# Longer pauses and finer steps for the lanes of small products in a two-layer hybrid backbone

## The chip, the cores and the metric

The kernel runs on one core of a Trainium2 chip. The metric is the device time of one execution in microseconds. Times shown are medians of a few runs; the profile is of one further execution of the same program.

## The reference

Two layers work on 1024 latent tokens and 256 context tokens of width 1024. The even layer runs latent attention (8 heads) and a chunked gated linear attention (GLA, 4 heads, both directions) side by side. The odd layer is a chunked gated DeltaNet (8 heads, both directions) with a short convolution of three taps on q, k and v. Each layer has modulated norms before both halves and a squared-ReLU MLP of width 4096. Cut to what the change touches:

```python
# GLA, per chunk of 64 and head (b = cumulative sum of the log gates)
q_dec, k_inv = q * exp(b), k * exp(-b)
a = where(incl, q_dec @ k_inv^T, 0);  o = a @ v + q_dec @ s
s = s * exp(b_end)[:, None] + (k * exp(b_end - b))^T @ v

# gated DeltaNet, per chunk of 64 and head
a_mat = where(strict, (k * beta) @ k^T * decay, 0) + eye(64)
sol = triangular_solve(a_mat, [v * beta, k * beta * exp(g)])

def rms_norm(x, w):
    return x * rsqrt(mean(x * x) + EPS) * w
```

## The kernel before

Large products run as three fp32r products per 128-wide contraction step (high by high, low by high, high by low; `mm3`, L180 to L183). `group` (L185) runs the eight steps of one 512-token block into one PSUM buffer. Its argument `every` says after how many microseconds of product columns it calls `pump`, at 1e9 once at the end of the group; `rate` scales the budget that `pump` hands on.

The rest of the work is written as generators, the lanes: GLA, norms, the feeders of the DeltaNet, the inversion of its triangular matrices. `lanes` (L58) lists them. `pump(us)` (L60) goes through the list, and each lane runs until what it yields adds up to the budget times its weight. A lane that yields `None` ends its turn for this call: that is a pause. What a lane records in its turn stands on each engine's queue at this place among the large products. The tile framework then orders the instructions of each engine; the order of the built program is shown below where it matters.

The places that the change touches:

- `stat_lane` (L233): squares (ScalarE), their sums, then a pause (L245), then the products `st` with a column of ones, then `rsqrt_small` on VectorE. `norm_lane` (L269) pauses once (L274) and then spreads the result with products `rb`.
- `gla_gates` (L333) computes gates on ScalarE, GpSimd and VectorE (a scan, L355), scales `gq` and `gk`, and transposes `gab` into `gkn` (L385). `gla_main` (L401) makes `pa` (L417), the state products `pk` (L435), the chain of states `gst` on VectorE (L439) and the outputs `po` (L457, L460). `gla_tail` (L473) normalises and transposes (L486). All of them share four PSUM buffers.
- In layer 1, `dense1` (L1136) runs the input projections. `conv_out` (L1164) accumulates the three taps on VectorE (L1174). `qk_lane` (L1189) transposes a projected block (L1198), normalises it, transposes it back (L1218) and stores it. `v_lane` (L1223) transposes (L1230) and stores.
- `decay_lane` (L1311) makes the decays of five sets of matrices with the products `pG` (L1327). `inv_lane` (L1358) makes the products `pk` (L1372), multiplies them on VectorE (L1375), and inverts the 32 by 32 diagonal blocks there: a transpose into `X` (L1390), thirty steps of two instructions that depend on each other (L1396, L1398), two transposes into `U` (L1407). `inv_tail` (L1420) joins the blocks with the products `pq` (L1429) and `pu` (L1441). These lanes share four PSUM buffers, tag `t`; the projections have four of their own.
- Five of the eight `gates` projections follow the last v block, then the lanes are drained, then three more `gates` projections cover the loads of the scan, whose first product is `pa` of L1628.

```python
            t += 3 * n / 2400
            if t >= every or k == nk - 1:
                pump(t * rate)
                t = 0.0
```

Of the kernel before, what the change touches and what calls it, by code (L numbers as in the profile page):

```python
# [33 lines left out]
def hybrid_backbone(ctx: ExitStack, tc: tile.TileContext, a, out, taps=None):  # L34
# [44 lines left out]
    def complete(gen):  # L79
        run(gen)  # L80
        lanes[:] = [it for it in lanes if it[0] is not gen]

    def run(gen):
# [149 lines left out]
    def stat_lane(hs, c0, n, tp, small, pp, ptag, dim, inc=False, engs=(V, G)):  # L233

        acc = []
        for i, h in enumerate(hs):
            sq = tp.tile([128, 512], F32, name="sq", tag="t")
            S.activation(out=sq[:, :n], in_=h[:, c0:c0 + n], func=AF.Square)
            if len(acc) < (1 if inc else 2) or (inc and i == len(hs) - 1):
                acc.append(sq)  # L240
            else:
                x = acc[0 if inc else i % 2]
                engs[i % 2].tensor_tensor(out=x[:, :n], in0=x[:, :n], in1=sq[:, :n], op=ALU.add)
            yield 0.4
        for _ in range(2 if inc else 1):  # L245
            yield None
        nt = n // 128
        st = pp.tile([128, 512], F32, name="st", tag=ptag)
        last = None
        for t in range(nt):  # L250
            for i, x in enumerate(acc):
                last = after(PE.matmul(st[:, t:t + 1], x[:, t * 128:(t + 1) * 128], ones, start=(i == 0), stop=(i == len(acc) - 1)), last)
        r = rsqrt_small(small, st[:, :nt], nt, dim)
        yield 1.2
        return r
# [13 lines left out]
    def norm_lane(hs, c0, n, A, B, dst, tp, small, pp, ptag, r=None, inc=False, rb=None, ks=range(KD)):  # L269

        c = 0 if c0 < LAT else 1
        if r is None and rb is None:
            r = yield from stat_lane(hs, c0, n, tp, small, pp, ptag, D, inc)
            yield None  # L274
        if rb is None:
# [125 lines left out]
    def gla_main(g):  # L401
# [3 lines left out]
        for h in range(4):  # L405
            while ("qk", h) not in gla:
                yield None
            qd, ki, v = gla["load", h]
            A_ = g.sb.tile([128, NT, 128], F32, name="gA")
            for t0 in (0, 4, 8):  # L410
# [18 lines left out]
            for s0 in (0, 8, 16):  # L429
                pk = [g.pp.tile([128, 4, 128], F32, name="pk", tag="p") for _ in range(2)]  # L430
                n = min(8, 19 - s0)
# [14 lines left out]
            ssq = g.sm.tile([128, NT], F32, name="gssq")  # L446
            yield None
            for t0 in (8, 0, 4):
# [24 lines left out]
    def gla_tail(g, h, o, ssq):  # L473
# [3 lines left out]
        yield 2.8  # L477
        yield None
        while ("gs", h) not in gla:
# [653 lines left out]
    with ExitStack() as e1:  # L1133
        pp = pool(e1, "pp1d", 4, space=PSUM)

        def dense1(chunks, blocks, rate=0.75, every=1e9, between=None):  # L1136
            ws = [w1s.pop() if w1s else load_w(a["owT"][m], wm[0], wbufs=2) for m, _ in chunks]
# [8 lines left out]
        with ExitStack() as e2:  # L1146
# [42 lines left out]
            def qk_lane(y, nt, gain, m, key):  # L1189

                yield None
                nat = cv.tile([128, NT, 128], F32, name="nat", tag="nat")
                ssq = small.tile([128, NT, 2], F32, name="ssq")
                for t0 in range(0, nt, 4):
# [6 lines left out]
                    S.activation(out=sq[:, :n], in_=pt[:, :n, :], func=AF.Square)  # L1201
                    V.tensor_reduce(out=ssq[:, t0:t0 + n], in_=sq[:, :n].rearrange("p t (a d) -> p t a d", a=2), axis=AX.X, op=ALU.add)
                r = rsqrt_small(small, ssq[:, :nt].rearrange("p t h -> p (t h)"), nt * 2, 1, gain)
                n3 = nat[:, :nt].rearrange("p t (a d) -> p (t a) d", a=2)
                V.tensor_tensor(out=n3, in0=n3, in1=r.unsqueeze(2).to_broadcast([128, nt * 2, 64]), op=ALU.mult)
                if key:
                    for p in range(2):
                        for a_ in range(2):
                            nc.sync.dma_start(out=d_X[m][64 * a_:64 * a_ + 64, p::2, 1, :],
                                              in_=nat[64 * p:64 * p + 64, :, 64 * a_:64 * a_ + 64])  # L1210
                for _ in range(3):
                    yield None
                xT = cv.tile([128, T], F32, name="xT", bufs=1)
                for t0 in range(0, nt, 4):
                    n = min(4, nt - t0)
                    pt = ptp.tile([128, 4, 128], F32, name="pt", tag="t")
                    for i in range(n):
                        PE.transpose(pt[:, i, :], nat[:, t0 + i, :], ident)  # L1218
                    S.copy(out=xT[:, t0 * 128:(t0 + n) * 128], in_=pt[:, :n, :].rearrange("p t f -> p (t f)"))
                nc.sync.dma_start(out=d_X[m][:, 0:2 * nt, 0 if key else 2, :], in_=xT[:, :nt * 128].rearrange("p (c j) -> p c j", j=64))  # L1220
                state[("k" if key else "q", m)] = True

            def v_lane(y, hh):  # L1223
                yield None
                vn = cv.tile([128, NT, 128], F32, name="vn", tag="nat")
                for t0 in range(0, NT, 4):
                    n = min(4, NT - t0)
                    pt = ptp.tile([128, 4, 128], F32, name="pt", tag="t")
                    for i in range(n):
                        PE.transpose(pt[:, i, :], y[:, tok(t0 + i)], ident)  # L1230
                    S.copy(out=vn[:, t0:t0 + n], in_=pt[:, :n, :])
                for p in range(2):
                    r0 = 64 * (hh % 2)
# [77 lines left out]
            def decay_lane():  # L1311

                for s, m in enumerate(sets):
# [3 lines left out]
                    for z in range(2):  # L1317
# [5 lines left out]
                        G.tensor_tensor(out=b4(R, m), in0=bc(g_, m), in1=i2b, op=ALU.mult)  # L1323
                        yield None
                        for i in range(2):
# [94 lines left out]
            def inv_tail(m, Nv, U, Y):  # L1420
                yield None
                yield None
                Q = [Nv[:, 16 * z:16 * z + 16, 0:32] for z in range(2)]
                for z in range(2):
# [6 lines left out]
                    for p in range(2):  # L1431
                        S.copy(out=Q[z][64 * p + 32:64 * p + 64], in_=pq[64 * p + 32:64 * p + 64])
                yield None
                for z in range(2):
# [408 lines left out]
```

## Time and profile before

| what | value |
|---|---|
| median of 3 runs | 3446.05 us (3445.41 to 3446.22) |
| the profiled execution's own time | 3441.82 us |
| its span in the profile | 3440.1 us |
| mean granted clock of TensorE | 0.97 |
| TensorE busy | 3264.4 us, 95% |
| VectorE busy | 2116.4 us, 62% |
| ScalarE busy | 1173.3 us, 34% |
| GpSimd busy | 1080.7 us, 31% |

The profiled execution's time exceeds its span by 1.7 us and lies 4.2 us under the median of the runs. The shares are means over stages that have different limits. Products are pipelined, and their ends are modelled: a product of 512 columns is shown with 0.39 us, while the next one starts after less. All times of the trace count from the start of the span.

### The profile page before, as it was taken

To read this page: it belongs to the slowest core of one execution; us is meant where nothing else is said; L and a number is where in the kernel's file an instruction comes from. 1 tells how busy PE (TensorE), PEld (TensorE's weight loads), DVE (VectorE), ACT (ScalarE), POOL (GpSimd) and SP (SyncE) were. 2 spreads that over 40 slices of the span, in tenths; PEclk is the share of its full clock that TensorE was granted. 3 is DMA by queue.
4 is the path that set the end of the run, shared out by engine and by line. 5 is a ranking of instruction groups with operands and counts; after the bars stand their busy time and mean duration, and the time that the engine had idled before them with its cause. 6 is when DMAs were issued, how large, how long until landed. Compare 5 with 4: busy or idle time off the path is not lost.

```text
span 3440.1 us, 48403 instructions
## 1 busy us (share of the span) xinstructions
PE 3264.4 (95%) x18676; PEld 2709.8 (79%) x18676; DVE 2116.4 (62%) x3873; ACT 1173.3 (34%) x2158; POOL 1080.7 (31%) x805
## 2 busy tenths in 40 slices
PE   8988988999899999999999898999999999999998
PEld 4876767777688888888888786777988788888887
DVE  4757446666568777776445779783765444444445
ACT  3234245665232212121212465452664311212112
POOL 2312136677442111111111343443117422222223
PEclk8998999999899999999999999999999999999999
DMA  5633132111622222222111234346454211111111
GB/s 197 197 101 90 59 120 72 29 47 29 203 80 77 86 70 85 69 91 59 49 37 38 74 93 103 92 121 155 104 111 148 68 49 43 49 50 48 43 51 62
DMA packets 284966, 287.86 MB, mean 84 GB/s; under 512 B 156424, under 2 KB 222032, under 8 KB 284736
## 3 DMA queue, kind: packets, MB, share of 16 engines
q1 hardware_dynamic: 272928, 263.53, 26.6%
q0 software_dynamic: 5760, 10.75, 1.3%
q10 hardware_dynamic: 6048, 10.49, 1.0%
q8 instruction: 147, 2.41, 0.3%
q14 instruction: 83, 0.68, 0.1%
HBM read 231.34 MB, written 53.36 MB: 83 GB/s over the span
## 4 chain that ended last, share of the span: by engine, by line
PE 69%; DVE 11%; DMA 3%; issue 2%; ACT 2%; POOL 2%; SPq 1%; DVEq 0%; ACTq 0%; POOLq 0%
PE ps L181 18%; PE ps L182 18%; PE ps L183 18%; DVE X L1398 1%; DVE tm L1396 1%; PE S L181 1%; PE S L182 1%; PE S L183 1%; DMA adaw<-in_adaw_dram 1%; PE pa L1645 1%; DVE y L1174 1%; PE acc L875 1%; PE acc L877 1%; PE acc L876 1%; PE M L857 1%
## 5 line engine op out<-in xcount | busy, mean ns | idle before, releaser
L170 POOL TENSOR_TENSOR wlo<-wst,whi 128x1024 fp32r<-128x1024 f32 (+1 forms) x207 | 489.8, 2374 | 1635.0 <-ACT whi L167 1587.9
L167 ACT CAST whi<-wst 128x1024 fp32r<-128x1024 f32 (+2 forms) x213 | 212.6, 1012 | 845.5 <-PE ps L182 771.8
L181 PE MATMUL ps<-th,whi 128*128 128x512 f32 (+1 forms) x1304 | 479.6, 368 | 7.0 <-DVE h L1068 5.4
L183 PE MATMUL ps<-th,wlo 128*128 128x512 f32 (+1 forms) x1304 | 476.3, 365 | 2.4 <-POOL wlo L170 2.4
L182 PE MATMUL ps<-tl,whi 128*128 128x512 f32 (+1 forms) x1304 | 477.5, 366 | 0.0
L1033 DVE TENSOR_TENSOR rl<-rl 128x512 f32<-128x512 f32 (+1 forms) x160 | 214.4, 1340 | 345.1 <-ACT rl L1032 344.5
L181 PE MATMUL ps<-mxh,whi 128*128 128x512 f32 (+1 forms) x1008 | 357.8, 356 | 0.0
L182 PE MATMUL ps<-mxl,whi 128*128 128x512 f32 (+1 forms) x1008 | 352.8, 350 | 0.3 <-POOL mxl L170 0.3
L183 PE MATMUL ps<-mxh,wlo 128*128 128x512 f32 (+1 forms) x1008 | 351.8, 350 | 0.0
L126 DVE SCALAR_TENSOR_TENSOR acc<-adaw,sc,acc 128x256 f32<-128x256 f32 (+1 forms) x476 | 286.2, 643 | 55.5 <-DMA adaw<-in_adaw_dram 55.4
L1068 DVE SCALAR_TENSOR_TENSOR h<-ps,mod,h 128x512 f32<-128x512 f32 (+1 forms) x384 | 243.5, 656 | 95.1 <-PE ps L183 93.7
L181 PEld LDWEIGHTS ps<-th,whi 128*128 128x128 f32 x1304 | 246.7, 189 | 51.0 <-DVE h L1068 7.2
L183 PEld LDWEIGHTS ps<-th,wlo 128*128 128x128 f32 x1304 | 246.3, 189 | 43.6 <-POOL wlo L170 3.2
L182 PEld LDWEIGHTS ps<-tl,whi 128*128 128x128 f32 x1304 | 246.9, 189 | 38.6
L1068 DVE SCALAR_TENSOR_TENSOR g<-ps,mod,g 128x512 f32<-128x512 f32 (+1 forms) x264 | 188.5, 731 | 106.3 <-PE ps L183 106.1
L181 PEld LDWEIGHTS ps<-mxh,whi 128*128 128x128 f32 x1008 | 195.2, 194 | 26.3 <-issue 1.2
L182 PEld LDWEIGHTS ps<-mxl,whi 128*128 128x128 f32 x1008 | 195.4, 194 | 25.8 <-issue 1.4
L183 PEld LDWEIGHTS ps<-mxh,wlo 128*128 128x128 f32 x1008 | 194.9, 194 | 23.9
L932 POOL TENSOR_TENSOR pl<-P,ph 128x512 fp32r<-128x512 f32 x144 | 178.6, 1247 | 89.9 <-DVE ph L931 60.1
L183 PE MATMUL ps<-m1h,wlo 128*128 128x512 f32 x512 | 203.9, 398 | 0.0
L181 PE MATMUL ps<-m1h,whi 128*128 128x512 f32 x512 | 203.9, 398 | 0.0
L182 PE MATMUL ps<-m1l,whi 128*128 128x512 f32 x512 | 203.6, 398 | 0.0
(376 smaller groups left out, 6725.5 us busy)
## 6 DMA issues: line engine op xcount, KB each, us to landing
wst<-in_w_dram SPq DMA_DIRECT2D x128, 512.0 KB, 3.5
adaw<-in_adaw_dram SPq DMA_DIRECT2D x224, 128.0 KB, 2.1
adaw<-in_adaw_dram SPq DMA_DIRECT2D x80, 256.0 KB, 4.5
wst<-in_owT_dram SPq DMA_DIRECT2D x25, 512.0 KB, 3.6
wst<-in_ewo_dram SPq DMA_DIRECT2D x16, 512.0 KB, 3.6
wY<-d_YA SPq DMA_DIRECT2D x64, 128.0 KB, 3.2
wst<-in_owo_dram SPq DMA_DIRECT2D x16, 512.0 KB, 3.5
wst<-in_ewT_dram SPq DMA_DIRECT2D x14, 512.0 KB, 7.1
```

Of the source, the lines that this page charges most:

```text
L126: V.scalar_tensor_tensor(out=acc[c], in0=w, scalar=sc[:, k, c:c + 1], in1=acc[c], op0=ALU.mult, op1=ALU.add)
L167: S.copy(out=hi, in_=src)
L170: lo_eng.tensor_tensor(out=lo, in0=src, in1=hi.bitcast(F32), op=ALU.subtract)
L181: PE.matmul(ps, hi_w, hi_x, start=first, stop=False)
L182: PE.matmul(ps, hi_w, lo_x, start=False, stop=False)
L183: PE.matmul(ps, lo_w, hi_x, start=False, stop=last)
L857: PE.matmul(ps[:, :kn_], qh[0:96, qt * 128:(qt + 1) * 128], kh[0:96, k0:k0 + kn_], start=True, stop=True)
L875: PE.matmul(o[:, :n], vh[:, j, :], ph[:, :n], start=(j == (0 if b < 2 else NTL)), stop=False, skip_group_check=True)
L876: PE.matmul(o[0:64, :n], vl[:, j, :], ph[:, :n], start=False, stop=False, skip_group_check=True)
L932: (V if j % 4 == 3 else G).tensor_tensor(out=pl[:, :n], in0=P_[:, :n], in1=ph[:, :n].bitcast(F32), op=ALU.subtract)
L1033: V.tensor_tensor(out=r[:, :n], in0=r[:, :n], in1=r[:, :n], op=ALU.mult)
L1068: V.scalar_tensor_tensor(out=h[m][:, c0:c0 + n], in0=ps[:, :n], scalar=mod[l][:, 40 + m, c:c + 1], in1=h[m][:, c0:c0 + n], op0=ALU.mult, o ...
```

## The change

A helper `pause(n)` yields `None` n times. Most lanes that wait for another engine's result before a product get more pauses than before. The transposes of `qk_lane` and `v_lane` end the lane's turn after each group of four. `dense1` pumps after every third contraction step of a 512-column group (its `every` is 1.6 where it was 1e9). The computation is the same.

```diff
+    def pause(n):
+
+        for _ in range(n):
+            yield None
...
@@ stat_lane
-        for _ in range(2 if inc else 1):
-            yield None
+        yield from pause(3 if inc else 2)
@@ norm_lane
             r = yield from stat_lane(hs, c0, n, tp, small, pp, ptag, D, inc)
-            yield None
+            yield from pause(3)
@@ gla_main
             qd, ki, v = gla["load", h]
+            yield from pause(4)
             A_ = g.sb.tile([128, NT, 128], F32, name="gA")
...
             ssq = g.sm.tile([128, NT], F32, name="gssq")
-            yield None
+            yield from pause(2)
@@ gla_tail
         yield 2.8
-        yield None
+        yield from pause(4)
@@ dense1
-        def dense1(chunks, blocks, rate=0.75, every=1e9, between=None):
+        def dense1(chunks, blocks, rate=0.75, every=1.6, between=None):
@@ qk_lane
-                yield None
+                yield from pause(3)
...
                     V.tensor_reduce(out=ssq[:, t0:t0 + n], in_=sq[:, :n].rearrange("p t (a d) -> p t a d", a=2), axis=AX.X, op=ALU.add)
+                    yield None
...
-                for _ in range(3):
-                    yield None
+                yield from pause(5)
...
                     S.copy(out=xT[:, t0 * 128:(t0 + n) * 128], in_=pt[:, :n, :].rearrange("p t f -> p (t f)"))
+                    yield None
@@ v_lane
-                yield None
+                yield from pause(3)
...
                     S.copy(out=vn[:, t0:t0 + n], in_=pt[:, :n, :])
+                    yield None
@@ decay_lane
-                        yield None
+                        yield from pause(2)
                         for i in range(2):
                             pG = ptp.tile([128, 8, 64], F32, name="pG", tag="t")
@@ inv_tail
-                yield None
-                yield None
+                yield from pause(4)
...
-                yield None
+                yield from pause(2)
                 for z in range(2):
                     pu = ptp.tile([128, 16, 32], F32, name="pu", tag="t")
```

How the order moves, at three places. Line numbers of the changed kernel lie 4 to 7 higher than before; the number at a tile's name tells buffers apart.

TensorE, the fifth and last set's `pq` in the layer-1 projections, in the kernel before:

```order
L183 MATMUL ps<-mxh_7_7179,wlo 128x512
L1429 MATMUL pq<-U_20985,Nm 32x32 x64
L181 MATMUL ps<-m0h_0_8096,whi 128x512
L1441 MATMUL pu<-U_20984,Nm 32x32
L182 MATMUL ps<-m0l_0_8104,whi 128x512
L183 MATMUL ps<-m0h_0_8096,wlo 128x512
L1441 MATMUL pu<-U_20984,Nm 32x32 x31
L1441 MATMUL pu<-Nm,U_20984 32x32 x32
```

The same place in the changed kernel:

```order
L188 MATMUL ps<-mxh_7_8087,wlo 128x256
L1435 MATMUL pq<-U_20690,Nm 32x32 x64
L186 MATMUL ps<-m0h_0_8096,whi 128x512
L187 MATMUL ps<-m0l_0_8104,whi 128x512
L188 MATMUL ps<-m0h_0_8096,wlo 128x512
```

Before, `pq` stands among the `gates` projections, with 144 dense products between it and the scan's first `pa`. Now it stands at the end of the seventh v block (a 256-column group ends in front of it), and 384 dense products and ten transposes of the eighth v block follow it.

VectorE, the end of the fourth set's inversion (`U`) and the start of the fifth's (`X`), in the kernel before:

```order
L1407 STREAM_TRANSPOSE U_20440<-X 128x32x32
L1407 STREAM_TRANSPOSE U_20439<-X 128x32x32
L1174 SCALAR_TENSOR_TENSOR y<-ps,cw,y 128x511 x2
L1174 SCALAR_TENSOR_TENSOR y<-ps,cw,y 128x1
L1174 SCALAR_TENSOR_TENSOR y<-edge,cw,y 128x1
L1174 SCALAR_TENSOR_TENSOR y<-ps,cw,y 128x255 x2
L1375 TENSOR_TENSOR Nm<-pk,Nm 128x512 x4
L1375 TENSOR_TENSOR Am<-pk,Am 128x512 x4
L1390 STREAM_TRANSPOSE X<-Nm 128x1024
```

The same place in the changed kernel:

```order
L1414 STREAM_TRANSPOSE U_20160<-X 128x32x32
L1414 STREAM_TRANSPOSE U_20159<-X 128x32x32
L1382 TENSOR_TENSOR Am<-pk,Am 128x512 x4
L1397 STREAM_TRANSPOSE X<-Nm 128x1024
L1179 SCALAR_TENSOR_TENSOR y<-ps,cw,y 128x511
L1403 TENSOR_TENSOR tm<-X 128x30
L1179 SCALAR_TENSOR_TENSOR y<-ps,cw,y 128x511
```

The fifth set's products `Nm` now stand ahead of the fourth set's `U`, and the convolution's rows stand between the steps of the fifth inversion.

TensorE, the first GLA head (`pa`, the transposes `pt<-gab`, the next head's gates `ps<-small_t`, `pk`), in the kernel before:

```order
L181 MATMUL ps<-a0h_0_145,whi 128x512
L417 MATMUL pa<-gq,gk 128x128 x20
L385 MATMUL pt<-ident,gab 128x128 x10
L342 MATMUL ps<-small_t,gu 128x512
L435 MATMUL pk<-gvt,gkn 64x128 x16
L342 MATMUL ps<-small_t,gu 128x512
L342 MATMUL ps<-small_t,gu 128x256
```

The same place in the changed kernel:

```order
L187 MATMUL ps<-a0l_2_155,whi 128x512
L389 MATMUL pt<-ident,gab 128x128 x10
L346 MATMUL ps<-small_t,gu 128x512 x2
L346 MATMUL ps<-small_t,gu 128x256
L422 MATMUL pa<-gq,gk 128x128 x20
L440 MATMUL pk<-gvt,gkn 64x128 x32
L188 MATMUL ps<-a0h_2_147,wlo 128x512
```

The whole place lies seven dense products later, the transposes and the next head's gates come first, and `pa` and 32 of the 38 `pk` follow without a dense product between.

## Rows read from the trace of the kernel before

**Rows 1.** The profile's page: busy us (share of the span) xinstructions of each engine.

```profile
PE 3264.4 (95%) x18676; PEld 2709.8 (79%) x18676; DVE 2116.4 (62%) x3873; ACT 1173.3 (34%) x2158; POOL 1080.7 (31%) x805
```

**Rows 2.** Windows by stage: length, busy us (x) per engine, granted clock, DMA.

```profile
core 0: us, PE busy (x) PEld busy (x) DVE busy (x) ACT busy (x) POOL busy (x), PEclk, DMA share, GB/s
200.00:410.00 210.00, 178.22 (x1467) 144.55 (x1466) 126.05 (x244) 80.59 (x101) 50.17 (x37) 0.89 0.28 80
1930.00:1960.00 30.00, 22.40 (x115) 19.17 (x114) 27.80 (x43) 15.50 (x24) 12.39 (x8) 0.83 0.30 103
1995.50:2054.80 59.30, 56.84 (x410) 47.64 (x411) 45.33 (x96) 34.87 (x57) 21.49 (x10) 1.00 0.35 89
1995.50:2346.20 350.70, 322.37 (x3010) 267.66 (x3011) 293.59 (x597) 176.25 (x274) 140.73 (x96) 0.97 0.42 105
```

**Rows 3.** TensorE's waits, 1995 to 2394 us: us in total, times, longest.

```profile
PE pt L1198 <- DVE Nm L1375: 6.6, 1, 6.6
```

**Rows 4.** TensorE's waits, 205 to 420 us, the four largest.

```profile
PE pt L486 <- DVE gst L439: 8.6, 2, 4.7
PE pa L417 <- issue: 8.2, 3, 4.4
PE pa L417 <- DVE gk L374: 5.6, 1, 5.6
PE po L457 <- DVE gst L439: 3.9, 1, 3.9
```

**Rows 5.** VectorE's waits, 1995 to 2346 us, all of them.

```profile
DVE y L1174 <- ACT y L1169: 13.4, 7, 4.5
DVE U L1407 <- POOL X L1402: 8.0, 4, 3.7
DVE Nm L1375 <- PE pk L1372: 7.8, 2, 4.4
DVE y L1174 <- ACT edge L1171: 7.2, 4, 3.4
DVE ssq L1202 <- ACT sqn L1201: 7.1, 3, 5.6
DVE X L1390 <- ACT Nm L1389: 2.9, 2, 1.6
DVE Am L1375 <- PE pk L1372: 1.0, 1, 1.0
```

**Rows 6.** Timeline of VectorE, end of the fifth inversion: start, us, instruction, idle before.

```profile
2342.01 4.17 DVE L1407 STREAM_TRANSPOSE U<-X 128x1024 f32<-128x1024 f32 x2 [3.70 <-POOL X L1402]
```

**Rows 7.** Timeline of TensorE from the fifth `pq` to the scan.

```profile
2356.72 2.21 PE L1429 MATMUL pq<-U,Nm 32*32 32x32 f32 x128
...
2362.16 0.50 PE L181 MATMUL ps<-m0h,whi 128*128 128x512 f32 x1
...
2394.29 0.39 PE L1628 MATMUL pa<-wv,wY 128*128 128x128 f32 x2
```

**Rows 8.** Timeline of VectorE: a step of the inversion and a convolution row behind it.

```profile
2286.70 0.19 DVE L1398 TENSOR_TENSOR X<-X,tm 128x30 f32<-128x30 f32 x1
2286.81 0.74 DVE L1174 SCALAR_TENSOR_TENSOR y<-ps,cw,y 128x511 f32<-128x511 f32 x1
```

**Rows 9.** Timeline of VectorE, first GLA head's states and the next head's scan.

```profile
253.49 2.82 DVE L355 TENSOR_TENSOR_SCAN gab<-cm,gmn 64x1280 f32<-64x1280 f32 x1 [3.33 <-POOL gmn L349]
256.23 0.32 DVE L439 SCALAR_TENSOR_TENSOR gst<-gst,ggi,pk 128x128 f32<-128x128 f32 x1
```

**Rows 10.** Timeline of TensorE, the norm between the layers.

```profile
1936.59 0.38 PE L252 MATMUL st<-ones,sq 128*128 128x1 f32 x2 [0.99 <-DVE sq L243]
...
1952.27 1.16 PE L261 MATMUL rb<-ident,rs_y 128*128 128x128 f32 x8 [3.19 <-DVE rs_y L215]
```

**Rows 11.** Timeline of TensorE: ten transposes; one set's `pk`.

```profile
1998.29 1.25 PE L1198 MATMUL pt<-ident,y 128*128 128x128 f32 x10
...
2046.43 3.95 PE L1372 MATMUL pk<-kq 64*64 64x64 f32 x128
```

## The prediction

> **What bounds the kernel now.** I read the busy shares first. TensorE is busy for 3264.4 of 3440.1 us [rows 1], so the most that a better order could return is the missing 176 us, and only in the stages that the change reaches. The windows by stage come next. The chunked-GLA stage (200 to 410 us) has TensorE busy 178 of 210 us at a granted clock of 0.89, that is, part of it at 1.2 GHz instead of 2.4. The projection and inversion stage of layer 1, from the first `pc` product at 1995.5 us to the scan, shows something else: until 2346.2 us VectorE is busy 293.6 of 350.7 us [rows 2]. The waits say who holds whom. In the GLA stage TensorE waits 31.5 us in nine kinds of wait, nearly all for the inputs or buffers of small products; the four largest, 26.3 us, are in [rows 4]. In the inversion stage its longest wait is 6.6 us [rows 3], about 29 us over 13 kinds. VectorE's own waits there are 13.4 + 8.0 + 7.8 + 7.2 + 7.1 + 2.9 + 1.0 = 47.4 us [rows 5]. So VectorE's instructions and the issue between them fill 350.7 - 47.4 = 303.3 us, and it is the next bound of this stage, not a helper with room.
>
> The end of the stage is read from the timeline. The last two transposes into `U` run on VectorE from 2342.01 for 4.17 us [rows 6]. TensorE takes the `pq` products that read them at 2356.72, ten us after: there TensorE is late, not VectorE. From `pq` to the scan's first `pa` (2394.29) are 37.57 us: 5.44 us of `pq` and `pu`, then 141 dense products in 32.13 us, 0.228 us each [rows 7].
>
> **The change, part by part.** No engine gains or loses an instruction of weight: 16106 products stand in both orders. Only places move.
>
> *Finer steps in `dense1` (L1136).* A pump now follows every third contraction step instead of a whole group, so three pumps where one was, and each may overrun its budget by one step. The lanes therefore advance faster per dense product than before, in spite of the longer pauses. In the two orders I count dense products of 512 columns: the fifth `pq` stands before the last 144 of them in the kernel before and before the last 384, with ten transposes, in the changed one. Since `pq` cannot start before the `U` transposes, 240 x 0.228 = 54.7 us and 1.25 us (ten transposes, [rows 11]) are moved behind VectorE's last inversion step: the tail grows from 37.6 to 93.5 us.
>
> When does that last step end? VectorE's queue in front of it loses only seven convolution rows (2.9 us at the 0.74 us of a 511-column one, [rows 8], less for the narrow ones). It also becomes better mixed: the chain of the inversion (L1396, L1398) is left for another instruction 70 times before, 126 times now. A convolution row behind a chain row starts at 2286.81, before the chain row's end at 2286.70 + 0.19 [rows 8], 0.08 us saved; 56 more of them save 4.5 us. VectorE's own need is then 303.3 - 2.9 - 4.5 = 295.9 us. (The Trainium skill, VectorE: DVE Perf Modes, section "The DRAIN you can't avoid", says that the next operation does not start until the pipe is empty, whatever is chained; by it the 4.5 us would be nothing and the sum 4.5 us longer. The row speaks for an overlap between independent operations.)
>
> To this come the waits that stay. In the first 59.3 us, until the first `X`, VectorE is busy only 45.3 [rows 2], which holds some 12 of its 47.4 us of waits; the first `pk` stands after 119 dense products instead of 164, ten us sooner, and VectorE's work ahead of it shrinks as much: I keep 10. Between the second `pq` and the third set's first `pk` TensorE has 50 dense products, `pq`, `pu` and 20 transposes, 11.5 + 5.4 + 2.5 us, then 3.95 us of `pk` [rows 11] and 2 us until `X`: 25 us, for which VectorE holds some 12: 13 of wait. Of the trips to GpSimd before `U` (8.0, [rows 5]) I keep 6, since nothing is put between. Sum 29, against 47.4 now. The last pair ends at 1995.5 + 295.9 + 29 = 2320.4, its first half 2.1 earlier, at 2318.3; plus the tail, 2411.8. TensorE waits ahead of `pq`, so some dense products will run at 1.2 GHz: 3 us. The stage ends at 2414.8 instead of 2394.3: **+20.5 us**. Bounds: if VectorE never waited, 2382.8, or -11.5, excluded by the 10 us at the start, so -1.5; if it waited as now, 2433, or +39. I take the middle value, because the order shows two of the three waits and not the rest.
>
> *Pauses in the GLA lanes (L409, L447, L478).* What the pauses delay is `pa`, `po` and the tail's transposes; `pt<-gab` (L385) has no pause and comes to stand first. For head 0 it needs `gab`, one product of 1.5 us after the `gk` that `pa` waits 5.6 us for [rows 4], and stands seven dense products (1.6 us) later: the wait changes its name, not its size. Then `po`: now it waits 3.9 us for `gst`, which stands on VectorE behind a scan that waits for GpSimd [rows 9]. In the new order both scans (2 x 2.8 us) stand ahead of all `gst` steps, so `pk`'s last six products, which need a buffer that the seventh `gst` step frees, would wait some 8 us: +4. For heads 1 to 3, `pa` (8.2 us, [rows 4]) gains cover in two of three cases (-4 us), and the transposes that waited 8.6 us stand behind fewer `pk` products (-6), but the third `pa` group of heads 1 and 2 needs buffers that VectorE frees only after the next head's scans (+2 to +5 each). With a little clock back I take **-4 us**. Bounds: all of the stage's 31.5 us and the lost clock (0.11 of 210 us) gone, -54; twice the scans' 5.6 us in the way, +15.
>
> *Pauses in the statistics lanes (L245, L274).* At 1936 to 1952 us `st` waits 0.99 and `rb` 3.19 us [rows 10]. Now 24 dense products (5.5 us) stand between them instead of 13 (3.0): `rb` keeps 0.7, `st` nothing, and less runs at the 0.83 clock [rows 2]: **-3 us** (-8 to +2, since the second `st` loses cover). The norm of layer 0's second block had no wait to lose; at the very end nothing dense is left to cover with: 0.
>
> *Pauses in the inversion and its feeders (L1191, L1211, L1224, L1324, L1421, L1433, and the three that split the transposes into groups of four)* act inside the sum of the stage above; alone they would push `pq` back, the wrong way only for the lanes' speed.
>
> **Sum:** 20.5 - 4 - 3 = +13.5 us. The profiled execution took 3441.82 us, so 3455; the median of the runs shown is 4.2 us above it, so the forecast in those terms is **3460 us** (+0.4%). A change under 0.2% (7 us) is about what a measurement of this kernel cannot tell from none.
>
> **The rivals.**
> 1. *Faster: the pauses cover what they were put in for, and VectorE keeps up.* It decides at the point where VectorE waits under 12 us in the inversion stage (the +20.5 falls to +3) while the GLA waits really go (-30 with their clock) and the norm's (-6): -33, 3413 us. For it: the GLA stage has 32 of 210 us without TensorE and a clock of 0.89 [rows 2]. Against it: 295.9 us of VectorE work and 93.5 us behind it, which no pause shortens. The Trainium skill (TensorE: Matmul & The Clock Gate, section "HAM oscillation") says that each wait puts the array back to half clock, so that a removed wait returns more than itself; the clock of 0.89 agrees, and by that rule this rival gains. Chance 0.17.
> 2. *No change:* the inversion stage loses 7 to 13 and GLA and norms return as much: 3440 to 3452 us, 0.15.
> 3. *Much slower:* VectorE waits as it does now (+39) and the scans block GLA (+10): 3492 us, 0.13.
> The forecast has 0.55. That the change does not do what it says is part of 2: in the GLA stage the small products still stand right behind their feeder.
>
> **How the numbers follow.** Slower by over 0.2%: 0.55 + 0.13 = 0.68; within: 0.15; faster: 0.17. The forecast's own range is 3453 to 3485 us. The range for 8 in 10 adds rival 2, the upper part of rival 1 and the lower part of rival 3: 3434 to 3492.
>
> **What would show it.** Right: in the changed profile the fifth `pq` starts right after the last `U`, between 2305 and 2345 us on this time axis, with TensorE idle for ten us or more in front of it or in front of transposes that wait for VectorE; VectorE's busy share before it is over 0.87; and some 90 us of nearly unbroken dense work follow, with VectorE nearly idle. Wrong: the last `U` ends before 2300 us, or `pq` does not wait. For GLA: the sum of waits between 200 and 410 us stays above 20 us and `pk` or `pt<-gab` heads the list. The prediction fails if the GLA stage gets shorter by over 15 us, or if VectorE's waits in the inversion stage fall under 15 us.

## The result and the profile after

The changed kernel takes 3465.24 us (median of 4 runs, 3462.31 to 3472.89), the kernel before beside it 3445.81 us (3445.41 to 3446.22). The ratio is 1.0069, 95% interval [1.0057, 1.0082]: slower by 0.7%. The profiled execution took 3465.45 us with a span of 3463.7, so 23.6 us more than the one shown before.

Where the time goes can be read by counting. The 12048 products of `mm3` stand in the same order in both kernels, so the start of the n-th one in one trace less its start in the other is the time lost or won up to there (`pc` and `pa` are the small products that begin the layer-1 stage and the scan):

```
place                                   before     after    shift
first product                             39.9      39.0     -0.9
product 1020, behind the GLA stage       500.2     492.9     -7.4
product 2160, second block's norm        973.0     962.4    -10.6
product 6900, end of layer 0's MLP      1915.2    1907.1     -8.1
first pc, start of the layer-1 stage    1995.5    1986.4     -9.1
first pa of the scan                    2394.3    2416.4    +22.1
last instruction                        3440.1    3463.7    +23.6
```

Everything ahead of the layer-1 projections got 9.1 us faster, and the stage from `pc` to the scan 31.2 us slower (430.0 against 398.8). The shares of the whole hardly tell it:

```profile
PE 3267.5 (94%) x18676; PEld 2709.9 (78%) x18676; DVE 2123.1 (61%) x3873; ACT 1171.3 (34%) x2154; POOL 1083.3 (31%) x805
```

The windows by stage do. First the whole stage in the kernel before, then three of the changed kernel: GLA, the layer-1 stage until the last `U`, and the whole stage. The columns are those of [rows 2].

```profile
1995.50:2394.29 398.79, 370.45 (x3457) 307.41 (x3458) 305.00 (x617) 189.47 (x294) 161.16 (x119) 0.97 0.45 110
```

```profile
200.00:410.00 210.00, 182.49 (x1513) 147.28 (x1512) 127.90 (x257) 81.34 (x104) 51.83 (x38) 0.89 0.28 80
1986.40:2322.60 336.20, 289.87 (x2799) 237.20 (x2800) 296.81 (x591) 165.17 (x254) 134.63 (x96) 0.91 0.40 96
1986.40:2416.40 430.00, 383.49 (x3451) 314.82 (x3452) 310.93 (x617) 189.88 (x292) 161.95 (x119) 0.93 0.41 101
```

In the whole stage TensorE is busy 13.0 us longer with the same products, at a granted clock of 0.93 instead of 0.97, and idle for 18.2 us more: that is the 31.2 us. VectorE is busy 88% until the last `U` and then 14 of 94 us. What TensorE waits for in the stage, the longest first (us in total, times, longest), to be held against [rows 3]:

```profile
PE pt L1236 <- ACT y L1186: 10.2, 1, 10.2
PE pk L1379 <- DVE X L1405: 8.3, 1, 8.3
PE pq L1435 <- DVE U L1414: 6.7, 2, 3.4
PE pt L1203 <- ACT sqn L1206: 4.7, 1, 4.7
PE pt L1203 <- ACT y L1186: 3.5, 2, 3.3
```

Before, no wait on this list ended with an instruction of the inversion (`X`, `U`); now 15 us do. The longest wait stands in front of the transposes of a v block, and the rows behind it show that the products that follow a wait are slower, too:

```profile
2213.77 1.11 PE L1236 MATMUL pt<-ident,y 128*128 128x128 f32 x4 [10.20 <-ACT y L1186]
2214.53 0.78 PE L186 MATMUL ps<-mxh,whi 128*128 128x512 f32 x1
2215.11 0.63 PE L187 MATMUL ps<-mxl,whi 128*128 128x512 f32 x1
2215.53 0.63 PE L188 MATMUL ps<-mxh,wlo 128*128 128x512 f32 x1
2215.96 0.63 PE L186 MATMUL ps<-mxh,whi 128*128 128x512 f32 x1
```

A dense product is shown with 0.63 us there, and the next one starts after 0.43 us (2215.53 to 2215.96) instead of 0.228: the clock is at 1.2 GHz. In the trace's record of the granted clock it was so for 24 us of the stage before and for 58 us of it now, and a stretch at 1.2 GHz follows each of the eight longest waits of the stage now. That agrees with the rule of the Trainium skill (TensorE: Matmul & The Clock Gate, "HAM oscillation") that was weighed in the prediction, with the sign turned round: here waits were added. VectorE's waits until the last `U`, to be compared with [rows 5], fell from 47.4 to 32.2 us; the first two are:

```profile
DVE y L1179 <- ACT edge L1176: 12.4, 2, 9.0
DVE ssq L1207 <- ACT sqn L1206: 7.1, 5, 2.3
```

The end of the stage, for [rows 6, 7]: the last two `U`, the fifth `pq`, the first dense product behind it, and the scan's `pa`.

```profile
2318.41 4.12 DVE L1414 STREAM_TRANSPOSE U<-X 128x1024 f32<-128x1024 f32 x2
```

```profile
2322.85 2.21 PE L1435 MATMUL pq<-U,Nm 32*32 32x32 f32 x128
2324.99 0.50 PE L186 MATMUL ps<-m0h,whi 128*128 128x512 f32 x1
...
2416.37 0.39 PE L1634 MATMUL pa<-wv,wY 128*128 128x128 f32 x2
```

`pq` starts 0.3 us after `U` ends, and 91.4 us of unbroken dense work follow it. But the row of `pq` has no idle time in front of it: TensorE came to this place just then.

In the GLA stage TensorE's waits changed their names more than their sum, 27.4 us against 31.5; the four largest now:

```profile
PE pk L440 <- DVE gst L444: 9.0, 1, 9.0
PE pk L440 <- DVE gA L424: 6.2, 2, 6.0
PE pt L389 <- DVE gab L381: 5.7, 1, 5.7
PE pa L422 <- DVE gA L424: 5.0, 1, 5.0
```

### The profile page after: what moved, and what is told of

The parts are those of the page before. It is cut to its first block, busy times and chain, and to the rows that moved or that the text cites. A ratio compares the mean times of both kernels' runs of the same rounds, so it can differ in the third digit from the quotient of the medians.

```text
span 3463.7 us, 48411 instructions
## 1 busy us (share of the span) xinstructions
PE 3267.5 (94%) x18676; PEld 2709.9 (78%) x18676; DVE 2123.1 (61%) x3873; ACT 1171.3 (34%) x2154; POOL 1083.3 (31%) x805
## 4 chain that ended last, share of the span: by engine, by line
PE 73%; DVE 14%; issue 4%; DMA 3%; ACT 3%; POOL 2%; SPq 1%; ACTq 0%; DVEq 0%; POOLq 0%
PE ps L186 18%; PE ps L187 18%; PE ps L188 18%; DVE X L1405 2%; DVE tm L1403 2%; DMA adaw<-in_adaw_dram 2%; DVE acc L131 1%; PE S L186 1%; PE S L187 1%; PE S L188 1%; DVE y L1179 1%; PE pa L1651 1%; PE acc L880 1%; PE acc L882 1%; PE acc L881 1%
```

## The experiments

Eleven further kernels ran, in three sets; each set shared its runs of the kernel before. On these chips the kernel before scattered more, from 3433 to 3452 us over 54 runs, so the ratios with their intervals and the length of the stage in the traces are what counts. One table for all of them: the stage from the first `pc` to the scan's `pa`, what TensorE is busy and idle in it, and, counted from `pc`, the end of the last `U`; the need is that length less VectorE's waits; "held" is the time by which VectorE's instructions there run longer than the median of their form in the same stage (those over 0.2 us), with their number. Where most rows of a form are stretched, so is their median, and "held" comes out too small: against the medians of all kernels together (those with `tm` in PSUM apart) it is 49.8 before, 61.5 in the changed kernel, 48.9 in e1, 45.5 in e6 and 44.1 in e10.

```
kernel                     ratio   stage  PE busy  idle  last U  need  held
before                     1       398.8  370.5    28.3   350.7  303.2  44.1 (26)
changed                    1.0069  430.0  383.5    46.5   336.2  304.1  60.6 (40)
e1 no layer-1 edits        0.9974  396.7  367.4    29.3   348.6  302.2  44.4 (26)
e2 steps only              1.0159  452.2  388.0    64.2   347.8  296.6  59.3 (38)
e3 rate 0.45               1.0016  410.1  374.6    35.5   354.0  307.8  53.7 (35)
e4 GLA pauses only         0.9985  401.8  373.1    28.7   353.7  304.0  44.4 (27)
e5 fifth pq late           1.0053  428.8  383.1    45.7   335.4  304.1  60.5 (39)
e6 tm in PSUM              1.0044  423.3  382.5    40.8   329.3  286.9  39.3 (35)
e7 pauses at the joins     1.0018  416.5  373.7    42.8   384.2  293.0  32.9 (20)
e8 products on VectorE     1.0051  418.7  383.4    35.3   331.9  295.0  34.2 (21)
e9 feeders, one more       0.9981  402.6  371.7    30.9   353.3  301.8  46.9 (30)
e10 e1 with tm in PSUM     0.9960  391.4  368.3    23.1   342.2  297.9  36.0 (25)
e11 e9 with tm in PSUM     0.9960  394.5  372.2    22.3   351.3  301.2  48.2 (32)
```

**e1, the layer-1 edits undone.** The changed kernel with `dense1`, `qk_lane`, `v_lane`, `decay_lane` and `inv_tail` as before:

```diff
-        def dense1(chunks, blocks, rate=0.75, every=1.6, between=None):
+        def dense1(chunks, blocks, rate=0.75, every=1e9, between=None):
...
-                yield from pause(3)
+                yield None
```

> The changed kernel with everything in the layer-1 projections put back (steps of dense1, feeders, decays, inv_tail), so only the pauses of GLA and of the statistics lanes stay. My theory: the whole loss lies in the layer-1 stage; ahead of it the trace of the changed kernel runs 13.0 us earlier than before at the same dense product, 3.3 us of small losses in between included. So 3446 - 13 = 3433 us, with the scan's first pa some 13 us earlier than before. Rival (the pauses of GLA and statistics push later work into worse places, and the loss is theirs too): 3446 or more.

Measured: 3433.46 us against 3441.21, ratio 0.9974 [0.9961, 0.9987]; the scan's `pa` comes 10.5 us earlier than in the kernel before. The loss lies in the layer-1 stage, and the pauses of GLA and of the statistics lanes alone make the kernel faster, by 8 us where 13 were expected. That the time itself met the expected 3433 is luck: the kernel before was 5 us faster in this set.

**e2, the finer steps alone.** The kernel before with one number changed:

```diff
-        def dense1(chunks, blocks, rate=0.75, every=1e9, between=None):
+        def dense1(chunks, blocks, rate=0.75, every=1.6, between=None):
```

> The kernel before with the finer steps of dense1 alone (every 1.6), no pause changed. The fifth pq then stands before the last 423 dense products, against 144 before and 384 in the changed kernel. My theory (steps let the lanes run ahead, pq waits for VectorE, the dense products behind it come too late): last U some 325 to 336 us after pc, tail 423 x 0.228 + 7 = 103 us, the stage 428 to 439 us against 398.8, so 3475 to 3486 us. Rival (the pauses of the feeders and of inv_tail make the loss): 3446 us, at most 3452. Rival (finer steps help VectorE, the loss is elsewhere): under 3446.

Measured: 3497.52 us, ratio 1.0159 [1.0142, 1.0177]. The steps make the loss, and more of it than expected: the stage grows by 53 us. The rival that blamed the pauses falls; they are worth 22 us in this stage once the steps are fine (430.0 against 452.2). TensorE's three longest waits stand ahead of the transposes back (for `nat`), the joins (for `U`) and a v block's transposes (for `y`):

```profile
PE pt L1218 <- DVE nat L1205: 23.9, 7, 7.9
PE pq L1429 <- DVE U L1407: 19.1, 4, 11.5
PE pt L1230 <- ACT y L1183: 10.8, 2, 9.6
```

**e3, fine steps at a slower pace.**

```diff
-        def dense1(chunks, blocks, rate=0.75, every=1.6, between=None):
+        def dense1(chunks, blocks, rate=0.45, every=1.6, between=None):
```

> The changed kernel, fine steps and all pauses kept, with the rate of dense1 at 0.45 instead of 0.75, so that the lanes advance about as slowly per dense product as before. The fifth pq stands before the last 222 dense products instead of 384. My theory: VectorE's last U comes 0 to 12 us later than the changed kernel's 336 us after pc, the tail shrinks by 162 x 0.228 = 37 us, so 3465 less 25 to 37: 3428 to 3440 us. Rival (fineness of the steps itself or the split transposes cost the time): 3455 to 3470 us.

Measured: 3448.9 us, ratio 1.0016 [1.0003, 1.0028]: a miss by 9 us over the upper end, between theory and rival. The pace gives back 20 of the 31 us of the stage (410.1) where 25 to 37 were expected, since VectorE is now fed later: its waits rise to 46.2 us and the last `U` comes 18 us later than in the changed kernel, not 0 to 12. What makes the 11 us that remain over the kernel before, whose VectorE waits as long (47.4 us), is not shown: TensorE is idle 7 us and busy 4 us longer, and the fine steps weren't separated from the pauses and the split transposes at this pace.

**e4, the GLA pauses alone** on the kernel before:

```diff
             qd, ki, v = gla["load", h]
+            yield from pause(4)
...
-            yield None
+            yield from pause(2)
...
-        yield None
+        yield from pause(4)
```

> The kernel before with the pauses of the GLA lanes alone. My theory: the trace of the changed kernel gains 7.5 us by the end of the GLA stage, and the statistics lanes add the rest of the 13.0; so 3446 - 7.5 = 3438.5 us (3437 to 3441), and the first run of this set lies some 5 us below it. Rival (the GLA gain is spent where layer 0's dense work waits for loads or for VectorE later on): 3444 to 3446.

Measured: 3436.31 us, ratio 0.9985 [0.9971, 0.9998]. In the trace the dense products behind GLA start 6.7 us earlier than before, where 7.5 were expected; the median gains 4.9. It lies 2.9 us over e1's; the intervals overlap, so the gain of the statistics lanes isn't settled by the times.

**e5, only the fifth `pq` put back** behind the dense products that it followed before:

```diff
             def inv_tail(m, Nv, U, Y):
-                yield from pause(4)
+                yield from pause(40 if m == sets[-1] else 4)
```

> The changed kernel with 40 pauses instead of 4 ahead of the last set's pq alone, so that it stands before the last 144 dense products again, as in the kernel before; all else as changed. Theory A (the prediction's working: what counts is how many dense products stand behind the last U): the stage loses most of the 54.7 us that 240 products take, 3465 - 40 to 55 = 3410 to 3425 us. Theory B (TensorE waited only 3.4 us at that pq; it is late there because each set's small products come early and wait for VectorE, 47.3 us in the stage against 28.2 before, and because the clock falls behind each wait): only those 3.4 us and a little clock return, 3460 to 3463 us.

Measured: 3460.0 us, ratio 1.0053 [1.0036, 1.007]; the stage is 1.2 us shorter. Theory A, the prediction's own picture, falls: what stands behind the last `U` is not lost because it stands there. By then TensorE has waited as long as in the changed kernel (45.7 us idle against 46.5), and it does all the dense products in any case:

```profile
PE pt L1236 <- ACT y L1186: 10.2, 1, 10.2
PE pk L1379 <- DVE X L1405: 8.3, 1, 8.3
PE pq L1435 <- DVE U L1414: 6.8, 2, 3.4
```

The 3.4 us of the expectation were put at the wrong `pq`: both waits stand in this kernel too, at the first and the second set's.

**e6, `tm` in PSUM.** VectorE's rows of the chain stretch at times. The timeline of VectorE in the changed kernel, and GpSimd's in the same stretch:

```profile
2198.61 0.41 DVE L1405 TENSOR_TENSOR X<-X,tm 128x238 f32<-128x238 f32 x1
2199.05 2.63 DVE L1403 TENSOR_TENSOR tm<-X 128x240 f32<-128x240 f32 x1
2201.72 2.48 DVE L1405 TENSOR_TENSOR X<-X,tm 128x240 f32<-128x240 f32 x1
2204.24 1.99 DVE L1403 TENSOR_TENSOR tm<-X 128x240 f32<-128x240 f32 x1
2206.15 0.74 DVE L1179 SCALAR_TENSOR_TENSOR y<-ps,cw,y 128x511 f32<-128x511 f32 x1
2206.81 1.44 DVE L1405 TENSOR_TENSOR X<-X,tm 128x240 f32<-128x240 f32 x1
```

```profile
2199.01 4.92 POOL L1359 TENSOR_TENSOR Am<-Nm,qmask 128x1024 f32<-128x1024 f32 x2 [7.71 <-ACT Nm L1344]
2203.90 4.08 POOL L1360 TENSOR_TENSOR Nm<-Nm,nbeta 128x1024 f32<-128x1024 f32 x2
```

A row of 0.41 us lasts until the GpSimd instruction beside it ends, while a convolution row, which reads `ps` from PSUM, keeps its 0.74 us. These rows also lead to TensorE's longest wait, the 10.2 us that end at 2213.77: it waits for `y`, which ScalarE finishes only when the convolution rows between the stretched ones are done, and ScalarE waits as long for them:

```profile
2211.36 1.28 ACT L1186 ACT_TABLE_LOAD   x1 [10.28 <-DVE y L1179]
```

The second longest, 8.3 us up to 2275.11, lies in the same way beside four rows that GpSimd's `Am` and `Nm` stretched by 6 us between 2264.81 and 2273.16. To see whether the operands decide how long a row is held:

```diff
-                    tm = iv.tile([128, 256], F32, name="tm")
+                    tm = ptp.tile([128, 512], F32, name="tm", tag="t")
```

> The changed kernel with the intermediate tm of the inversion's chain in one of the four PSUM buffers of the lanes instead of SBUF. Then the sums X (L1405) read one SBUF operand and one PSUM operand, the products tm (L1403) still two SBUF operands. In the changed kernel 40 VectorE instructions of the stage run 60.6 us longer in all than the median of their form, 29 of them rows of the chain, all while a GpSimd instruction runs. Theory (GpSimd holds a VectorE instruction that reads two SBUF operands until its own ends): no X row is held any more, tm rows are, held time falls from 60.6 to 35 to 45 us, VectorE's need in the stage by as much less what PSUM reads cost; the time 3445 to 3465 us, with one lane buffer fewer working against it. Rival (the long rows are something else, say an access conflict on the output): X rows still stretch as often as tm rows, held time 55 us or more.

Measured: 3458.17 us, ratio 1.0044 [1.0028, 1.0059]. VectorE's two groups of the chain until the last `U` (busy us, mean ns of one), first of the changed kernel, then of this one:

```profile
L1405 DVE TENSOR_TENSOR X<-X,tm 128x30 f32<-128x30 f32 (+9 forms) x150 | 74.4, 496 | 2.9
L1403 DVE TENSOR_TENSOR tm<-X 128x30 f32<-128x30 f32 (+9 forms) x150 | 70.5, 470 | 3.1
```

```profile
L1403 DVE TENSOR_TENSOR tm<-X 128x30 f32<-128x30 f32 (+9 forms) x150 | 78.7, 525 | 2.7
L1405 DVE TENSOR_TENSOR X<-X,tm 128x30 f32<-128x30 f32 (+9 forms) x150 | 48.4, 323 | 2.7
```

Of the 150 `X` rows 15 were stretched, now none; of the `tm` rows 14, now 25 (by the medians of the three kernels with `tm` in PSUM). So in the chain it is the second SBUF operand. This agrees with the Trainium skill (SBUF — State Buffer, "SBUF: two separate sides"), which says that VectorE with two SBUF inputs and GpSimd reading SBUF exclude each other for a whole instruction. VectorE's need falls by 17 us, the stage by 6.7; VectorE's waits rise by 10 us meanwhile, and what the lane buffer that `tm` takes away costs by itself was not tried.

**e7, the pauses at the joins with whole groups.** e1 with the pauses of `decay_lane` (2) and `inv_tail` (4 and 2):

```diff
             def inv_tail(m, Nv, U, Y):
-                yield None
-                yield None
+                yield from pause(4)
```

> The first run's kernel (pauses of GLA and statistics lanes) with the pauses of the decays and of inv_tail added, dense1 at whole groups as before. The five pq stand behind 410, 590, 830, 1046 and 1151 of 1190 dense products, against 374, 530, 710, 902 and 1046 in the first run's kernel. Theory (TensorE's small products should stand behind VectorE's results): its waits in the stage fall from 30.0 to 15 to 22 us, the stage from 396.7 to 384 to 392 us, the whole 5 to 12 us under the first run's kernel, some 0.5% to 0.65% under the kernel before in all. Rival (VectorE is the bound, later pk make it wait): last U 10 us or more later than 348.6 us after pc, and no gain.

Measured: 3449.12 us, ratio 1.0018 [1.0005, 1.0031]. The rival was right, and the delay larger than it said: VectorE waits 91 us, the last `U` comes 36 us later than in e1, and only 39 dense products are left behind the fifth `pq`. Then the scan waits:

```profile
2402.42 0.77 PE L1632 MATMUL pa<-wv,wY 128*128 128x128 f32 x2 [13.08 <-DMA wv<-d_v]
```

From the last `U` to this `pa` are 32.3 us, of which the dense products covered too little. Some dense work behind the last `U` is needed for the joins, the stores and the loads.

**e8, GpSimd's products on VectorE.**

```diff
-                            G.tensor_tensor(out=Am[:, z], in0=Nm[:, z], in1=qmask[:, z:z + 1, :].to_broadcast([128, 16, 64]), op=ALU.mult)
+                            V.tensor_tensor(out=Am[:, z], in0=Nm[:, z], in1=qmask[:, z:z + 1, :].to_broadcast([128, 16, 64]), op=ALU.mult)
-                        G.tensor_tensor(out=b4(Nm[:, z], m), in0=b4(Nm[:, z], m), in1=bc(blocks_of(nbeta, z, m), m), op=ALU.mult)
+                        V.tensor_tensor(out=b4(Nm[:, z], m), in0=b4(Nm[:, z], m), in1=bc(blocks_of(nbeta, z, m), m), op=ALU.mult)
```

> The changed kernel with GpSimd's 18 products Am and Nm (L1359, L1360) done by VectorE. In the changed kernel these 18 hold VectorE's rows for 29.1 us of the 60.6 us; before, they held them for 14.3 of 44.1. On VectorE they should take 1.1 to 1.3 us each (the 128x1024 product nat takes 1.22), 21.6 us in all. Theory (a GpSimd product under the chain costs VectorE about as much as doing it itself): VectorE's need in the stage 304.1 - 29.1 + 21.6 = 297 us, held time near 31 us, the whole 3455 to 3466 us. Rival (GpSimd's work is free for VectorE, the long rows have another cause): held time stays at 50 to 60 us, VectorE's need grows to 320 us or more, the whole 3475 us or more.

Measured: 3460.12 us, ratio 1.0051 [1.0031, 1.0071]. Held time is 34.2 us, VectorE's need 295.0; TensorE's idle time in the stage falls from 46.5 to 35.3 us and the stage by 11.3. The products take 21.8 us there:

```profile
L1360 DVE TENSOR_TENSOR Nm<-Nm,nbeta 128x1024 f32<-128x1024 f32 x10 | 12.1, 1214 | 0.0
L1359 DVE TENSOR_TENSOR Am<-Nm,qmask 128x1024 f32<-128x1024 f32 x8 | 9.7, 1216 | 0.0
```

On GpSimd they took 40.3 us and held VectorE for 29.1 of them, so in the changed order the helper's work cost VectorE more than doing it itself.

**e9 to e11, towards a faster kernel.** e9 is e1 with one more pause ahead of the feeders' transposes, e10 is e1 with `tm` in PSUM, e11 has both:

```diff
             def v_lane(y, hh):
-                yield None
+                yield from pause(2)
```

> The first run's kernel (pauses of GLA and statistics lanes, dense1 at whole groups) with one more pause, two instead of one, at the start of qk_lane and of v_lane. TensorE waits 6.6 + 5.3 + 4.5 us there for rows of the convolution before the lanes' first transposes. Theory (a pause of one more whole group, 24 dense products or 5.5 us, covers a wait of that size, and the places of the last three pq stay): waits of the stage fall from 30 to 16 to 22 us, the stage from 396.7 to 386 to 393 us, the whole 0.35% to 0.55% under the kernel before. Rival (the later feeders delay VectorE's pk, as the pauses of the joins did, and the waits come back as waits for U): stage 397 us or more, the whole at most 0.25% under the kernel before.

> The first run's kernel with tm in PSUM; TensorE's order is the same, only VectorE's rows get shorter where GpSimd held them. In the first run's kernel 44.4 us are held in the stage. Theory: held time falls to 25 to 32 us and VectorE's need by 10 to 18 us, but TensorE reached the fifth pq 10 us after the last U already, so only its waits for VectorE's results (some 12 of 30 us) can return: the stage 388 to 395 us against 396.7, the whole 0.3% to 0.5% under the kernel before. Rival (one lane buffer fewer makes TensorE's small products wait for buffers): stage 397 us or more.

> Both of the two kernels ahead together. Theory: the gains add up where they remove different waits, the stage 380 to 390 us against 396.7, the whole 0.45% to 0.75% under the kernel before. Rival (they remove the same waits, or the later feeders meet the missing buffer): not faster than the better of the two.

Measured: e9 3437.84 us, ratio 0.9981 [0.9969, 0.9993]: no better than e1, its stage 5.9 us longer. The rival's figures hold, its reason doesn't: no wait for `U` came back, but 6.6 us ahead of a `pk`, and 5.5 of the 6.6 us that the pause was to cover stayed. e10 3430.93 us, 0.9960 [0.9945, 0.9974], stage 391.4 as expected, though VectorE's need falls by 4.3 us only (10 to 18 expected). e11 3431.8 us, 0.9960 [0.9944, 0.9976]: no faster than the better of the two, as its rival said. e10 has the shortest stage of all and is faster than the kernel before and the changed one; that it beats e1 isn't settled, the intervals overlap. Its window of the stage:

```profile
1990.60:2382.00 391.40, 368.31 (x3451) 305.94 (x3452) 300.18 (x618) 190.37 (x294) 158.62 (x119) 0.98 0.45 112
```

All pauses with whole groups in `dense1` weren't tried in one kernel.

## Why the prediction was right, and where its steps were not

The forecast was 3460 us, slower by 0.4%; 3465 us and 0.7% came. The range held it, and the likeliest case, with its place, was the one that happened. That the two times lie only 5 us apart is in part luck: the sum was 10 us short, and the 4.2 us added because the profiled execution lay under its median were not needed after the change, where it lay on it. Step by step, in the profiled execution (+23.6 us where the sum said +13.5):

- **The inversion stage, forecast +20.5, measured +31.2.** This is the term that was mis-sized. The last `U` was to come 324.9 us after `pc` and came after 336.2. Of these 11 us, 3 are waits (32.2 instead of 29: 12.9 for the 10 kept, 18.1 for the 13, 0.8 for the 6) and 8 VectorE's need, 304.1 instead of 295.9. The forecast let the need fall with the convolution rows and the better mixing, and without the held time it did fall, by 11 us or more; what it didn't price is that GpSimd's instructions now run beside the chain. Held time went from 44.1 to 60.6 us (49.8 to 61.5 by the common medians), and the products `Am` and `Nm` alone hold 29.1 us instead of some 13. e6 and e8 show this cause, and TensorE's two longest waits lie beside rows held in this way.
- **The picture behind this term was wrong in part.** "240 x 0.228 = 54.7 us ... are moved behind VectorE's last inversion step" gave the right length of the tail (93.5 us from `pq` to `pa`, as forecast), but not the cause: e5 moved them back and won 1.2 us, so that the term came near is partly luck. TensorE itself is late at that place, after 46.5 us without work in the stage and 58 us at half clock. The ten idle us that the prediction named as a sign stood ahead of a v block's transposes, and none ahead of the fifth `pq`. The step that held is the one before: lanes that advance faster per dense product put their products ahead of VectorE's results. e2 shows that the finer steps do it, e3 that the pace is most of it (20 of 31 us).
- **"TensorE waits ahead of `pq`"** was to cost 3 us of clock, a term that no row stood behind. It was more: busy time rose by 13.0 us for the same products, with 58 us at 1.2 GHz instead of 24.
- **GLA, forecast -4, measured -7.4** at product 1020, of which 0.6 us stood ahead of the stage. The names were right: `pk` behind `gst` 9.0 us (8 forecast), `pt<-gab` 5.7 where `gk` had 5.6. The waits of `pa`, `po` and the tail's transposes fell by 23 us, and the new ones cost 19. The parts that the prediction lists add up to between -2 and +4, so its -4 rested on an unpriced gain of clock; the clock was at 1.2 GHz for 41 us of the stage before and after, and 2.4 us of busy time were won.
- **Statistics, forecast -3, measured -1.0** up to `pc`, which stands six dense products (1.4 us) later now. The waits were not covered: `rb` waits 6.9 us at its longest instead of 3.2 [rows 10], while a wait of 3.0 us for `h` is gone. The count under this term was wrong: between `st` and `rb` stood 24 products of 256 columns and 9 of 512 before, worth 21 of the latter and not 13, and 30 and 9 stand there now, worth 24. At the second block of layer 0, forecast 0, 3.3 us were won; 2.6 us were lost up to the end of layer 0's MLP, most of it in two waits for `h` (2.2 us instead of 0.8, 1.0 instead of none); no edit stands there, and the cause stays open.
- **Behind the scan's start, forecast 0:** +1.5 us, 0.9 of it in the wait of `pa` for `sg` (7.3 instead of 6.4).
- **The 16106 products** that the prediction counts in both orders are 18676 in both profiles; nothing hangs on it, since the number did not change.

Rival 1 failed by the condition it was given, VectorE's waits at 32.2 us instead of under 12, and its GLA term of -30 was 7. Without the layer-1 edits its direction is right: e1 is faster than before, by 8 us and not by 33.

## What to carry to other kernels

When small products are interleaved with dense ones, finer steps and longer pauses act here on one thing, how far the small products run ahead of the engine that feeds them: too early, and TensorE waits, 64 us of the stage, and its clock falls (e2); too late, and the feeder waits, 91 us, and nothing covers the end (e7). Change one of them in a stage where the feeder is itself near its bound only with the pace re-tuned, and judge the stage by TensorE's idle time and busy time, not by what is left behind the feeder's last result. Count what a helper engine costs its neighbour before calling its work free (e8).

## What was not expected of the hardware

A VectorE instruction of the chain, with two SBUF operands, lasts until the GpSimd product that it meets ends: 0.41 us became 2.63 us beside a product of some 2.4 us. 29 rows of the chain were held in this way in one stage, 46.4 of the 60.6 us. With one operand in PSUM none of 150 was stretched (e6), and those that stay exposed meet GpSimd oftener instead, 25 rows for 14. A fill by GpSimd (`MEMSET`, 2.19 us for four at 2307.13 us) left the rows of the chain beside it at 0.35 to 0.37 us.

Two SBUF operands are not the only case. Among the other 11 rows are two of `rsqrt_small` that read a single tensor, from SBUF. One of them, 0.18 us in the median, lasted until the GpSimd product beside it ended; why such a row is held was not tried:

```profile
2030.42 1.45 DVE L210 TENSOR_SCALAR rs_m<-ssq 128x20 f32<-128x20 f32 x1
```

```profile
2029.45 2.38 POOL L175 TENSOR_TENSOR wlo<-wst,whi 128x1024 fp32r<-128x1024 f32 x1 [8.82 <-ACT whi L172]
```
